# A transformer layer with 16384 experts: pools of its own for the first half of the expert blocks

## The chip, the cores and the metric

The kernel runs on one core of a Trainium2 chip. The metric is the device time of one execution in microseconds (us). Engines are named as in the profile: PE (TensorE; PEld is its weight load), DVE (VectorE), ACT (ScalarE), POOL (GpSimd) and SP (SyncE, here only an issuer of DMAs).

## The reference, cut to what matters

One layer over 1024 tokens of width 1024: two kinds of attention, an output projection, a LayerNorm, then PEER, a layer of 16384 experts of one neuron each, and a second LayerNorm. The change lies in PEER:

```python
def peer(x, w_q, sub_keys, u, v):
    q = (xf @ w_q).reshape(n, PEER_HEADS, 2, PEER_QDIM // 2)
    sc = jnp.einsum('nhpc,hpkc->nhpk', q, sub_keys)
    s_top, i_top = lax.top_k(sc, PEER_TOPK)                 # 16 of 128 keys, twice per head
    ...                                                     # 16 of the 16 x 16 sums
    g = jax.nn.softmax(fs, axis=-1)
    h = jnp.einsum('cd,chkd->chk', xc, u[ec])
    a = jax.nn.gelu(h, approximate=False) * gc
    return jnp.einsum('chk,chkd->cd', a, v[ec])
```

## The kernel before, in words

The tokens lie in eight tiles of 128. Attention, projection and LayerNorm run pair by pair of tiles, each pair followed by `route(pr)`, which finds the experts of its two tiles: transposes of x1 (L529) into `th` and `tl` (L530, L531; an fp32 value is carried as a high and a low half, so that a product takes three matmuls), then 16 steps over c, each with 24 matmuls into the PSUM tile `pq` (L555 to L557), a copy `q` (L559), two matmuls with the keys (L562), a copy `sc` (L564) and the selection of 16 on DVE. Each step loads its halves of the query weights by SP (`qhi`, L551). `decode` then works out expert numbers and gates on DVE (L179 to L235; `eidx` L224).

PEER itself is computed in two ways. **Tiles 5 to 7 are gathered**: 384 gathers by POOL (L656), each followed by a dot product (L658) and an accumulation (L668) on DVE. **Tiles 0 to 4 (640 tokens) are computed densely** over all experts, in 128 blocks of 128. Their gates must first stand in DRAM as a full table: POOL scatters those of tiles 0 and 1 (L165, into `gs`), and `build` makes those of tiles 2 to 4 by matmuls of one-hot rows (`pi`, `qj`, `pr`, `stage`, L602 to L617, into `gd`).

A dense block e is `hstage`: load `raw` from `ut[e]` (L709), split it into `uh` (ACT, L86) and `ul` (DVE, L87), 48 matmuls 128x320 in two runs of 24 into the one PSUM tile `h` (L91 to L93), a gelu of each run into `gl` (ACT, L718), a product of `gl` with the gates `gt` (DVE, L722), a split into `ah` and `al`, a load of `vt` into `raw` and its split into `vh` and `vl`. Then follow 18 matmuls 128x512 into `po` for tiles 0 to 2 (`vres`) and, for two blocks together, 24 into `fl` for tiles 3 and 4 (`vflush`), added to `facc` on DVE (L760, L765). `pump` spreads the gathers over the blocks.

The program text is not the order of the work. A scheduler (Tile) places each instruction in its engine's queue by its own estimate of times, and an engine runs its queue in order. What it may move is limited by buffers: the pool `dn` and the PSUM pool `ph`, which hold everything of the dense stage, take space that the pools of attention and `route` (closed by `late.close()` and the end of their block) held until then.

```python
    dn = ctx.enter_context(tc.tile_pool(name="dn", bufs=2))
    ph = ctx.enter_context(tc.tile_pool(name="ph", bufs=1, space=PSUM))
    ...
        raw = dn.tile([P, KT, P], F32, name="raw", bufs=3)
    ...
        gl = dn.tile([P, DN], F32, name="gl")
```

Of the kernel before, what the change touches and what calls it, by code (L numbers as in the profile page):

```python
# [11 lines left out]
F32 = mybir.dt.float32  # L12
F32R = mybir.dt.float32r
# [6 lines left out]
PSUM = bass.MemoryType.PSUM  # L20

P = 128
S = 1024
D = 1024
KT = D // P
# [11 lines left out]
GBUF = 4  # L37
ND = 5
NG = NT - ND
DN = ND * P  # L40
# [17 lines left out]
def trunk(ctx, tc, x, xt, wqk, wo, gn, sink, biasa, biasb, ln, wq, keyst, uv, ut, vt, out):  # L58
# [22 lines left out]
    def load_ln(g):  # L81
        for i in range(2):
            nc.scalar.dma_start(lnt[:, i, :], bcast_rows(ln[2 * g + i], D))

    def split(hi, lo, raw, lo_eng=None):
        cp = nc.scalar.copy(hi, raw)  # L86
        nc.vector.tensor_sub(lo, raw, f(hi))  # L87
        return cp

    def mm3(ps, wh, wl, mh, ml, first, last):  # L90
        nc.tensor.matmul(ps, wh, mh, start=first, stop=False)  # L91
        nc.tensor.matmul(ps, wh, ml, start=False, stop=False)  # L92
        nc.tensor.matmul(ps, wl, mh, start=False, stop=last)  # L93
# [538 lines left out]
    dl = dx.tile([P, KT, DN], F32R, name="dl")  # L632
    nc.sync.dma_start(f(dh), xd[0])
    nc.sync.dma_start(f(dl), xd[1])
    x1p = ctx.enter_context(tc.tile_pool(name="x1p", bufs=2, side="right"))
    x1 = {}
    load_ln(1)
    gp = ctx.enter_context(tc.tile_pool(name="gp", bufs=GBUF, side="right"))
    ga = ctx.enter_context(tc.tile_pool(name="ga", bufs=1, side="right"))
    sm = ctx.enter_context(tc.tile_pool(name="sm", bufs=2))  # L640

    def residual_ln(t, r, tmp):
# [35 lines left out]
    def pump(n):  # L678
        while n > 0 and done[0] < total:
            next(gen)  # L680
            done[0] += 1
            n -= 1

    dn = ctx.enter_context(tc.tile_pool(name="dn", bufs=2))
    ph = ctx.enter_context(tc.tile_pool(name="ph", bufs=1, space=PSUM))
    RES = 3
    po = [ph.tile([P, 2, 512], F32, name=f"po{c}") for c in range(RES)]
# [3 lines left out]
    xr = {}  # L691
# [4 lines left out]
    def load_g(g):  # L696
        gt[g] = dn.tile([P, DN // GC, EG, GC], F32, name="gt")
        sl = slice(g * EG, (g + 1) * EG)
        ns = NS * P // GC
        ld = nc.sync.dma_start(gt[g][:, 0:ns], gv[:, :, sl, :].rearrange("q j i c -> j q i c"))  # L700
        for t in range(NS):
            for b in added[t, 7]:
                tc.add_manual_dep(ld.ins, b.name, SYNC, reason="gates of every head")
        if NS < ND:
            nc.sync.dma_start(gt[g][:, ns:], gd[:, :, sl, :].rearrange("q j i c -> j q i c"))

    def hstage(e, pend):
        raw = dn.tile([P, KT, P], F32, name="raw", bufs=3)
        nc.sync.dma_start(raw, ut[e])  # L709
        uh = dn.tile([P, KT, P], F32R, name="uh")  # L710
        ul = dn.tile([P, KT, P], F32R, name="ul")
        split(uh, ul, raw)
        gl = dn.tile([P, DN], F32, name="gl")
        for j, (o, n) in enumerate(hch):
            ps = ph.tile([P, 512], F32, name="h")
            for k in range(KT):
                mm3(ps[:, :n], uh[:, k, :], ul[:, k, :], dh[:, k, o:o + n], dl[:, k, o:o + n], k == 0, k == KT - 1)
            nc.scalar.activation(gl[:, o:o + n], ps[:, :n], AF.Gelu)  # L718
            if j == (e == ne - 1) and pend is not None:
                vres(*pend)  # L720
        glv = gl.rearrange("p (q c) -> p q c", c=GC)
        nc.vector.tensor_mul(glv, glv, gt[e // EG][:, :, e % EG, :])  # L722
        ah = dn.tile([P, DN], F32R, name="ah", bufs=3)
        al = dn.tile([P, DN], F32R, name="al", bufs=3)
        split(ah, al, gl)
        raw = dn.tile([P, D], F32, name="raw", bufs=3)
        nc.sync.dma_start(raw, vt[e * P:(e + 1) * P, :])
        vh = dn.tile([P, D], F32R, name="vh", bufs=3)
        vl = dn.tile([P, D], F32R, name="vl", bufs=3)
        split(vh, vl, raw)  # L730
        return ah, al, vh, vl

    def vmm(ps, c, j, a, first, last):
        ah, al, vh, vl = a
        cs, js = slice(c * P, (c + 1) * P), slice(j * 512, (j + 1) * 512)
        nc.tensor.matmul(ps, ah[:, cs], vh[:, js], start=first, stop=False)  # L736
        nc.tensor.matmul(ps, ah[:, cs], vl[:, js], start=False, stop=False)  # L737
        nc.tensor.matmul(ps, al[:, cs], vh[:, js], start=False, stop=last)  # L738
# [3 lines left out]
    def vres(e, a):  # L742
        for c in range(RES):
            for j in range(2):
                vmm(po[c][:, j, :], c, j, a, e == 0, e == ne - 1)

    def vflush(e, a):
        prev.append(a)
        if len(prev) == 2:
            for c in range(RES, ND):  # L750
                acc = facc[c - RES]
                if e == 1:
                    xr[c] = dn.tile([P, D], F32, name="raw", bufs=3)
                    nc.scalar.dma_start(xr[c], xs[c])
                for j in range(2):
                    ps = ph.tile([P, 512], F32, name="fl")
                    for n, b in enumerate(prev):
                        vmm(ps, c, j, b, n == 0, n == 1)
                    if e == 1:
                        nc.vector.scalar_tensor_tensor(acc[:, j, :], xr[c][:, j * 512:(j + 1) * 512], ALPHA, ps,  # L760
                                                       op0=OP.mult, op1=OP.add)
                    else:
                        fl = dn.tile([P, 512], F32, name="fl", bufs=2)
                        nc.scalar.copy(fl, ps)  # L764
                        nc.vector.tensor_add(acc[:, j, :], acc[:, j, :], fl)  # L765
            prev.clear()

    fed = 0
    pend = None
    load_g(0)  # L770
    for e in range(ne):
        if e % EG == 0 and e + EG < ne:
            load_g(e // EG + 1)
        a = hstage(e, pend)
        if pend is not None:
            vflush(*pend)
        pend = (e, a)
        while fed < min(total, total * (e + 4) // ne):
            pump(1)
            fed += 1  # L780
    vres(*pend)
    vflush(*pend)
    pump(total)
    for c in range(ND):
# [78 lines left out]
```

## Time and profile before

| | us |
|---|---|
| median of 3 runs (lowest to highest) | 2982.5 (2979.24 to 2985.24) |
| the profiled execution | 2985.32 |
| its span in the trace | 2981.6 |
| PE busy / DVE busy / ACT busy / POOL busy | 2733.9 / 2408.1 / 1202.3 / 1065.1 |
| first matmul into `h` starts | 1133.34 |
| last matmul ends | 2961.9 |

The profiled execution's own time is 3.7 above its span. Busy time says how long an engine executed something, not whether anyone waited for it; for that the views of waits, the chain that ended last and the timelines are read, stage by stage. Times of instructions count from the start of the span.

### The profile page before, as it was taken

The page shows a single profiled execution, that of the slowest core. Times are in us where ns is not written, and L with a number is a line of the kernel's source. Part 1 is how long each engine was busy: PE and PEld are TensorE (multiplying, and loading weights), DVE is VectorE, ACT ScalarE, POOL GpSimd, SP SyncE. Part 2 cuts the span into 40 slices and gives each one's busy share as a digit, 9 for nine tenths or more (in the row PEclk, how much of TensorE's full clock was granted, in tenths as well). Part 3 has the DMA queues.
Part 4 walks back from the last instruction along what each step waited for, and adds up shares of the span by engine and source line. Part 5 has one row for each costly group of instructions (what it writes and reads, how often), then busy time and mean ns, then how long its engine had stood idle before and what let it go on. Part 6 is the DMA issues. An engine that isn't in the chain of part 4 may idle for free.

```text
span 2981.6 us, 43327 instructions
## 1 busy us (share of the span) xinstructions
PE 2733.9 (92%) x15569; PEld 2357.3 (79%) x15569; DVE 2408.1 (81%) x5427; ACT 1202.3 (40%) x2486; POOL 1065.1 (36%) x732
## 2 busy tenths in 40 slices
PE   6887899897997867999999999999999999999996
PEld 4776577575785766888998899898888898988885
DVE  2344267887979988898998989999989999998965
ACT  2343154342786762333333343333333333333332
POOL 1111001078888881333333323333333333333300
PEclk8998989898997988999999999999999999999998
DMA  7688598897977767988998989998998898998851
GB/s 233 200 271 269 177 322 296 260 262 180 267 223 221 220 161 265 348 331 324 353 331 332 332 329 335 336 347 334 330 344 327 321 353 322 342 349 332 329 210 46
DMA packets 384886, 854.37 MB, mean 287 GB/s; under 512 B 83616, under 2 KB 243360, under 8 KB 333728
## 3 DMA queue, kind: packets, MB, share of 16 engines
q0 software_dynamic: 124224, 433.43, 41.3%
q1 hardware_dynamic: 230816, 388.82, 38.5%
q10 hardware_dynamic: 29632, 29.37, 3.1%
q8 instruction: 122, 2.00, 0.3%
q14 instruction: 92, 0.75, 0.1%
HBM read 765.21 MB, written 86.11 MB: 286 GB/s over the span
## 4 chain that ended last, share of the span: by engine, by line
PE 48%; DVE 5%; DMA 4%; issue 3%; ACT 2%; POOL 1%; SPq 0%; ACTq 0%; POOLq 0%; DVEq 0%
PE h L91 9%; PE h L92 8%; PE h L93 8%; PE po L736 5%; PE po L737 5%; PE po L738 5%; PE fl L737 3%; PE fl L736 3%; PE fl L738 3%; DMA uv<-in_uv_dram,eidx 2%; DMA raw<-in_ut_dram 2%; DVE uv L658 1%; DVE acc L668 1%; POOL uv L656 1%; DVE vl L87 1%
## 5 line engine op out<-in xcount | busy, mean ns | idle before, releaser
L656 POOL DMA_INDIRECT uv<-in_uv_dram,eidx x384 | 570.4, 1486 | 1162.5 <-DVE acc L668 688.5
L91 PE MATMUL h<-dh,uh 128*128 128x320 f32 x2048 | 641.3, 313 | 49.0 <-ACT uh L86 25.6
L93 PE MATMUL h<-dh,ul 128*128 128x320 f32 x2048 | 634.6, 310 | 0.8 <-DVE ul L87 0.8
L92 PE MATMUL h<-dl,uh 128*128 128x320 f32 x2048 | 634.1, 310 | 0.0
L658 DVE SCALAR_TENSOR_TENSOR uv<-uv,xg 128x1024 f32<-128x1024 f32 x384 | 467.4, 1218 | 43.1 <-DMA uv<-in_uv_dram,eidx 37.3
L165 POOL DMA_INDIRECT gs<-gated,idxd x256 | 434.9, 1699 | 171.3 <-DMA qlo<-wqd 87.0
L668 DVE SCALAR_TENSOR_TENSOR acc<-uv,hh,acc 128x1024 f32<-128x1024 f32 x381 | 487.6, 1280 | 4.3
L91 PEld LDWEIGHTS h<-dh,uh 128*128 128x128 f32 x2048 | 385.7, 188 | 83.7 <-ACT gl L718 48.6
L92 PEld LDWEIGHTS h<-dl,uh 128*128 128x128 f32 x2048 | 385.9, 188 | 10.9
L93 PEld LDWEIGHTS h<-dh,ul 128*128 128x128 f32 x2048 | 385.7, 188 | 4.9 <-DVE ul L87 1.5
L736 PE MATMUL po<-vh,ah 128*128 128x512 f32 x768 | 288.2, 391 | 1.5 <-ACT ah L86 1.5
L737 PE MATMUL po<-vl,ah 128*128 128x512 f32 x768 | 287.8, 391 | 0.0
L662 ACT ACTIVATE hh<-hh 128x1 f32<-128x1 f32 x384 | 77.6, 202 | 476.3 <-DVE uv L658 474.9
L738 PE MATMUL po<-vh,al 128*128 128x512 f32 x768 | 260.8, 391 | 0.0
L764 ACT COPY fl<-fl 128x512 f32<-128x512 f32 x252 | 147.1, 584 | 278.7 <-PE fl L738 278.5
L765 DVE TENSOR_TENSOR facc<-facc,fl 128x512 f32<-128x512 f32 x252 | 172.6, 685 | 72.8 <-ACT fl L764 72.6
L718 ACT ACTIVATE gl<-h 128x320 f32<-128x320 f32 x256 | 111.4, 435 | 254.5 <-PE h L93 244.4
L736 PE MATMUL fl<-vh,ah 128*128 128x512 f32 x512 | 201.8, 394 | 3.0 <-ACT fl L764 3.0
L737 PE MATMUL fl<-vl,ah 128*128 128x512 f32 x512 | 201.9, 394 | 0.0
L738 PE MATMUL fl<-vh,al 128*128 128x512 f32 x512 | 199.6, 390 | 0.0
L87 DVE TENSOR_TENSOR ul<-raw,uh 128x1024 fp32r<-128x1024 f32 x128 | 156.1, 1220 | 52.6 <-ACT uh L86 51.7
L86 ACT CAST uh<-raw 128x1024 fp32r<-128x1024 f32 x128 | 134.2, 1049 | 116.8 <-DMA raw<-in_ut_dram 60.7
(201 smaller groups left out, 5389.2 us busy)
## 6 DMA issues: line engine op xcount, KB each, us to landing
raw<-in_ut_dram SPq DMA_DIRECT2D x128, 512.0 KB
raw<-in_vt_dram SPq DMA_DIRECT2D x128, 512.0 KB
qhi<-wqd SPq DMA_DIRECT2D x48, 512.0 KB
qlo<-wqd SPq DMA_DIRECT2D x48, 512.0 KB
gd<-stage SPq DMA_DIRECT2D x12, 2048.0 KB
gt<-gd SPq DMA_DIRECT2D x32, 768.0 KB
wraw<-in_wqk_dram SPq DMA_DIRECT2D x36, 512.0 KB
bt<-in_biasb_dram SPq DMA_DIRECT2D x64, 288.0 KB
```

Source lines behind the costliest of these rows:

```text
L87: nc.vector.tensor_sub(lo, raw, f(hi))
L91: nc.tensor.matmul(ps, wh, mh, start=first, stop=False)
L92: nc.tensor.matmul(ps, wh, ml, start=False, stop=False)
L93: nc.tensor.matmul(ps, wl, mh, start=False, stop=last)
L165: st = nc.gpsimd.indirect_dma_start(out=gs, out_offset=bass.IndirectOffsetOnAxis(ap=idx[:, k:k + 1], axis=0), in_=g[:, k:k + 1], in_offset ...
L656: nc.gpsimd.indirect_dma_start(out=u, out_offset=None, in_=uv, in_offset=bass.IndirectOffsetOnAxis(ap=eidx[t][:, k:k + 1], axis=0))
L658: nc.vector.scalar_tensor_tensor(u[:, 0:D], u[:, 0:D], 1.0, x1[t], op0=OP.mult, op1=OP.mult, accum_out=hh[:, k:k + 1])
L668: nc.vector.scalar_tensor_tensor(acc, u[:, D:], hh[:, k:k + 1], acc, op0=OP.mult, op1=OP.add)
L736: nc.tensor.matmul(ps, ah[:, cs], vh[:, js], start=first, stop=False)
L737: nc.tensor.matmul(ps, ah[:, cs], vl[:, js], start=False, stop=False)
L738: nc.tensor.matmul(ps, al[:, cs], vh[:, js], start=False, stop=last)
L765: nc.vector.tensor_add(acc[:, j, :], acc[:, j, :], fl)
```

## The change

The loads of `ut`, the halves `uh` and `ul` and the gelu results `gl` go from `dn` into a pool `du` that is allocated right behind `dh` and `dl` (the halves of the dense tiles' x, which are loaded behind `route(2)`; `load_ln` and the rest of the dense stage follow in the text), and the sums `h` go into a PSUM pool `hb` of one bank, both ahead of the remaining pools. `gl` has three buffers in place of two; `raw` has three as before. The four other pools get `reuse_waits="tile"`: a tile waits for the earlier tiles whose space it takes, not for the whole of the earlier pool. The first load of `ut` is written ahead of the gates' first load, and later gate loads behind `hstage`.

```diff
--- before.py
+++ after.py
@@ -632,11 +632,13 @@
     dl = dx.tile([P, KT, DN], F32R, name="dl")
     nc.sync.dma_start(f(dh), xd[0])
     nc.sync.dma_start(f(dl), xd[1])
-    x1p = ctx.enter_context(tc.tile_pool(name="x1p", bufs=2, side="right"))
+    du = ctx.enter_context(tc.tile_pool(name="du", bufs=2))
+    hb = ctx.enter_context(tc.tile_pool(name="hb", bufs=1, space=PSUM))
+    x1p = ctx.enter_context(tc.tile_pool(name="x1p", bufs=2, side="right", reuse_waits="tile"))
     x1 = {}
     load_ln(1)
-    gp = ctx.enter_context(tc.tile_pool(name="gp", bufs=GBUF, side="right"))
-    ga = ctx.enter_context(tc.tile_pool(name="ga", bufs=1, side="right"))
+    gp = ctx.enter_context(tc.tile_pool(name="gp", bufs=GBUF, side="right", reuse_waits="tile"))
+    ga = ctx.enter_context(tc.tile_pool(name="ga", bufs=1, side="right", reuse_waits="tile"))
     sm = ctx.enter_context(tc.tile_pool(name="sm", bufs=2))
 
     def residual_ln(t, r, tmp):
@@ -681,7 +683,7 @@
             done[0] += 1
             n -= 1
 
-    dn = ctx.enter_context(tc.tile_pool(name="dn", bufs=2))
+    dn = ctx.enter_context(tc.tile_pool(name="dn", bufs=2, reuse_waits="tile"))
     ph = ctx.enter_context(tc.tile_pool(name="ph", bufs=1, space=PSUM))
     RES = 3
     po = [ph.tile([P, 2, 512], F32, name=f"po{c}") for c in range(RES)]
@@ -704,15 +706,18 @@
         if NS < ND:
             nc.sync.dma_start(gt[g][:, ns:], gd[:, :, sl, :].rearrange("q j i c -> j q i c"))
 
-    def hstage(e, pend):
-        raw = dn.tile([P, KT, P], F32, name="raw", bufs=3)
+    def load_u(e):
+        raw = du.tile([P, KT, P], F32, name="raw", bufs=3)
         nc.sync.dma_start(raw, ut[e])
-        uh = dn.tile([P, KT, P], F32R, name="uh")
-        ul = dn.tile([P, KT, P], F32R, name="ul")
+        return raw
+
+    def hstage(e, pend, raw):
+        uh = du.tile([P, KT, P], F32R, name="uh")
+        ul = du.tile([P, KT, P], F32R, name="ul")
         split(uh, ul, raw)
-        gl = dn.tile([P, DN], F32, name="gl")
+        gl = du.tile([P, DN], F32, name="gl", bufs=3)
         for j, (o, n) in enumerate(hch):
-            ps = ph.tile([P, 512], F32, name="h")
+            ps = hb.tile([P, 512], F32, name="h")
             for k in range(KT):
                 mm3(ps[:, :n], uh[:, k, :], ul[:, k, :], dh[:, k, o:o + n], dl[:, k, o:o + n], k == 0, k == KT - 1)
             nc.scalar.activation(gl[:, o:o + n], ps[:, :n], AF.Gelu)
@@ -723,7 +728,7 @@
         ah = dn.tile([P, DN], F32R, name="ah", bufs=3)
         al = dn.tile([P, DN], F32R, name="al", bufs=3)
         split(ah, al, gl)
-        raw = dn.tile([P, D], F32, name="raw", bufs=3)
+        raw = du.tile([P, D], F32, name="raw", bufs=3)
         nc.sync.dma_start(raw, vt[e * P:(e + 1) * P, :])
         vh = dn.tile([P, D], F32R, name="vh", bufs=3)
         vl = dn.tile([P, D], F32R, name="vl", bufs=3)
@@ -750,7 +755,7 @@
             for c in range(RES, ND):
                 acc = facc[c - RES]
                 if e == 1:
-                    xr[c] = dn.tile([P, D], F32, name="raw", bufs=3)
+                    xr[c] = du.tile([P, D], F32, name="raw", bufs=3)
                     nc.scalar.dma_start(xr[c], xs[c])
                 for j in range(2):
                     ps = ph.tile([P, 512], F32, name="fl")
@@ -767,11 +772,12 @@
 
     fed = 0
     pend = None
+    first = load_u(0)
     load_g(0)
     for e in range(ne):
+        a = hstage(e, pend, load_u(e) if e else first)
         if e % EG == 0 and e + EG < ne:
             load_g(e // EG + 1)
-        a = hstage(e, pend)
         if pend is not None:
             vflush(*pend)
         pend = (e, a)
```

Three places show what this moves. The first is PE's queue at the start of `route(3)`: `x_10242` is the x1 of tile 6, whose transposes (L529) open that route; `pr` are the matmuls of `build`. Before:

```order
L615 MATMUL pr<-pi,qj 128x128 x35
L529 MATMUL pq<-ident,x_10242 128x128 x2
L615 MATMUL pr<-pi,qj 128x128
L529 MATMUL pq<-ident,x_10242 128x128 x2
L615 MATMUL pr<-pi,qj 128x128 x4
L529 MATMUL pq<-ident,x_10242 128x128 x4
L615 MATMUL pr<-pi,qj 128x128 x4
L529 MATMUL pq<-ident,x_10244 128x128 x4
L615 MATMUL pr<-pi,qj 128x128 x8
L529 MATMUL pq<-ident,x_10244 128x128 x4
```

Now:

```order
L615 MATMUL pr<-pi,qj 128x128 x28
L91 MATMUL h<-dh,uh 128x320
L92 MATMUL h<-dl,uh 128x320
L615 MATMUL pr<-pi,qj 128x128 x6
L529 MATMUL pq<-ident,x_10242 128x128 x4
L615 MATMUL pr<-pi,qj 128x128 x2
L93 MATMUL h<-dh,ul 128x320
L91 MATMUL h<-dh,uh 128x320
L92 MATMUL h<-dl,uh 128x320
L93 MATMUL h<-dh,ul 128x320
```

Matmuls into `h` (blocks 0 to 2, 144 in all) now stand between the transposes, the last 48 of them between the first and the third of the 16 steps over c; from the third step on both programs interleave `pr` and `pq` alike.

The second place is DVE's queue in the decode of tile 6 (L215 to L221 belong to it, L126 to L230 with numbers to tile 7's selection), shortly before the dense stage. Before:

```order
L215 TENSOR_TENSOR pf<-pf,of 128x128
L126 MATCH_REPLACE t_11330<-fs,cv 128x50
L126 MATCH_REPLACE t_11336<-fs,cv 128x50
L217 SCALAR_TENSOR_TENSOR big<-pf,fi 128x128 x8
L127 MAX fs<-t_11330 128x8
L127 MAX fs<-t_11336 128x8
L221 TENSOR_REDUCE ef<-big 128x128
L128 MAX_INDEX pos<-fs,t_11330 128x8
L128 MAX_INDEX pos<-fs,t_11336 128x8
L230 TENSOR_TENSOR gate_107<-fs 128x128
```

Now:

```order
L215 TENSOR_TENSOR pf<-pf,of 128x128
L87 TENSOR_TENSOR vl<-raw,vh 128x1024
L126 MATCH_REPLACE t_11330<-fs,cv 128x50
L126 MATCH_REPLACE t_11336<-fs,cv 128x50
L217 SCALAR_TENSOR_TENSOR big<-pf,fi 128x128 x8
L87 TENSOR_TENSOR vl<-raw,vh 128x1024
L127 MAX fs<-t_11330 128x8
L127 MAX fs<-t_11336 128x8
L87 TENSOR_TENSOR vl<-raw,vh 128x1024
L221 TENSOR_REDUCE ef<-big 128x128
L727 TENSOR_TENSOR gl<-gl,gt 128x640 x3
L128 MAX_INDEX pos<-fs,t_11330 128x8
```

The `vl` of blocks 0 to 2, the products of `gl` with the gates and the `al` have moved into this stretch; the `ul` of blocks 0 to 2, which followed some rows below, have gone to the start of `route(3)`.

The third place is PE's queue where the dense stage starts, behind the last 40 matmuls of `build`. Before:

```order
L615 MATMUL pr<-pi,qj 128x128 x3
L562 MATMUL pq<-kt,q 128x128 x2
L615 MATMUL pr<-pi,qj 128x128 x40
L91 MATMUL h<-dh,uh 128x320
L92 MATMUL h<-dl,uh 128x320
L93 MATMUL h<-dh,ul 128x320
```

Now:

```order
L615 MATMUL pr<-pi,qj 128x128 x3
L562 MATMUL pq<-kt,q 128x128 x2
L615 MATMUL pr<-pi,qj 128x128 x40
L741 MATMUL po_11454<-vh,ah 128x512
L742 MATMUL po_11454<-vl,ah 128x512
L741 MATMUL po_11455<-vh,ah 128x512
L742 MATMUL po_11455<-vl,ah 128x512
L741 MATMUL po_11456<-vh,ah 128x512
L742 MATMUL po_11456<-vl,ah 128x512
```

Where 72 matmuls into `h` stood first, `po` and `fl` of block 0 come first now. On SP, the loads `u`, `v`, `u` of blocks 0, 0 and 1 stand directly behind those of `dh` and `dl`, and `v`, `u`, `v` of blocks 1, 2 and 2 ahead of the `qhi` that `route(3)` loads for its third step (c = 2); the gate loads stand where they stood.

## Rows read from the trace of the kernel before

**Rows 1.** The page, part 1: engine, busy us, share, instructions.

```profile
PE 2733.9 (92%) x15569; PEld 2357.3 (79%) x15569; DVE 2408.1 (81%) x5427; ACT 1202.3 (40%) x2486; POOL 1065.1 (36%) x732
```

**Rows 2.** Windows: stretch, busy us per engine, granted clock, DMA share, GB/s.

```profile
940.00:980.00 40.00, 25.48 (x123) 22.91 (x123) 38.87 (x117) 29.82 (x68) 33.01 (x18) 0.60 0.57 157
980.00:1090.00 110.00, 91.89 (x713) 86.38 (x711) 94.53 (x368) 81.35 (x201) 93.96 (x53) 1.00 0.77 224
1110.00:1130.00 20.00, 0.00 (x0) 0.00 (x0) 20.00 (x99) 0.31 (x1) 5.83 (x4) 0.50 0.85 237
1200.00:2860.00 1660.00, 1640.02 (x9125) 1477.77 (x9124) 1515.49 (x2210) 595.24 (x1198) 554.17 (x372) 1.00 0.91 336
```

**Rows 3.** PE timeline, 1133 to 1164: start, us, instruction, idle before.

```profile
1133.34 0.64 PE L91 MATMUL h<-dh,uh 128*128 128x320 f32 x1 [25.65 <-ACT uh L86]
...
1139.04 0.47 PE L91 MATMUL h<-dh,uh 128*128 128x320 f32 x1
1139.30 0.42 PE L92 MATMUL h<-dl,uh 128*128 128x320 f32 x1
...
1139.70 0.31 PE L91 MATMUL h<-dh,uh 128*128 128x320 f32 x1
1139.85 0.31 PE L92 MATMUL h<-dl,uh 128*128 128x320 f32 x1
...
1149.59 0.39 PE L736 MATMUL po<-vh,ah 128*128 128x512 f32 x1
...
1154.38 0.30 PE L91 MATMUL h<-dh,uh 128*128 128x320 f32 x1
...
1163.24 0.39 PE L736 MATMUL po<-vh,ah 128*128 128x512 f32 x1
```

**Rows 4.** Chain that ended last, 1114 to 1133: start, us, what.

```profile
1114.59 4.18 DMA gs<-gated,idxd
1119.07 0.37 SPq L700
...
1124.24 7.67 DMA raw<-in_ut_dram
1132.25 1.05 ACT uh L86
```

**Rows 5.** DVE timeline, 1120 to 1149.

```profile
1120.09 0.26 DVE L215 TENSOR_TENSOR pf<-pf,of 128x128 f32<-128x128 f32 x1
...
1120.64 1.68 DVE L217 SCALAR_TENSOR_TENSOR big<-pf,fi 128x128 f32<-128x128 f32 x8
...
1122.49 1.84 DVE L221 TENSOR_REDUCE ef<-big 128x128 f32<-128x1024 f32 x1
...
1135.88 1.21 DVE L87 TENSOR_TENSOR vl<-raw,vh 128x1024 fp32r<-128x1024 f32 x1
...
1147.42 0.83 DVE L722 TENSOR_TENSOR gl<-gl,gt 128x640 f32<-128x640 f32 x1
```

**Rows 6.** ACT timeline, 969 to 971 and 1148.

```profile
969.64 1.28 ACT L231 ACT_TABLE_LOAD   x1
970.94 0.31 ACT L231 ACTIVATE gate<-gate 128x128 f32<-128x128 f32 x1
...
1148.28 0.73 ACT L86 CAST ah<-gl 128x640 fp32r<-128x640 f32 x1 [2.37 <-DVE gl L722]
```

**Rows 7.** PE waits, 930 to 980: for whom, us, times, longest.

```profile
PE pr L615 <- ACT qj L611: 16.5, 9, 5.7
```

**Rows 8.** PE timeline, first steps of route(3).

```profile
977.76 0.36 PE L555 MATMUL pq<-th,qhi 128*128 128x256 f32 x1
...
989.70 0.38 PE L555 MATMUL pq<-th,qhi 128*128 128x256 f32 x1 [0.46 <-ACT sc L564]
```

**Rows 9.** PE waits, 1200 to 2860.

```profile
PE h L91 <- ACT gl L718: 18.3, 32, 2.0
```

**Rows 10.** The page, part 5: DVE waiting for gathered rows.

```profile
L658 DVE SCALAR_TENSOR_TENSOR uv<-uv,xg 128x1024 f32<-128x1024 f32 x384 | 467.4, 1218 | 43.1 <-DMA uv<-in_uv_dram,eidx 37.3
```

## Prediction

> **What bounds the kernel now.** The page first: PE is busy 2733.9 of 2981.6 us [rows 1], so it is the engine to follow, and the question is where its other 248 us lie. The windows by stage tell that [rows 2]. From 1200 to 2860, over half of the run, PE is busy 1640.0 of 1660: the dense stage is bound by PE, and its idle 20.0 us are nearly all one wait, the first matmul of a run of 24 into `h` waiting for the gelu that empties the one `h` bank, 32 times, 18.3 us [rows 9], 0.57 each. Ahead of it PE does nothing at all in 1110 to 1130, while DVE is busy for all of it and PE's granted clock is 0.50 of full speed [rows 2]. In 940 to 980, where `route(3)` begins, PE is busy 25.5 of 40 us, DVE 38.9, ACT 29.8 [rows 2]; PE waits there 16.5 us for `qj`, which ACT scales [rows 7]. From 980 to 1090 PE is busy 91.9 of 110.
>
> The timeline shows the hole before the dense stage: the first matmul into `h` starts at 1133.34 after 25.65 idle, released by the split `uh` [rows 3]. The chain that ended last tells why it is so late [rows 4]: the last scatter of gates lands (4.18), SP then issues the gates' loads (1119.07), behind these in SP's queue the load of the first `u` (1124.24, 7.67 to its landing), then `uh` (1132.25, 1.05). Dense matmuls can't start before, though `dh`, `dl` and `u` need none of what `route(3)` computes: the buffers are what holds them.
>
> **What the change moves: the gain.** The matmuls into `h` of three blocks, 144, now stand in PE's queue at the start of `route(3)`; the dense stage opens with `po` and `fl`. A matmul into `h` takes 0.147 at full clock (1139.70 to 1139.85) and 0.267 at half (1139.04 to 1139.30) [rows 3]; three blocks are 144 x 0.147 = 21.2 us of PE's work.
>
> When can `po` of block 0 start? It needs `vl`, the gated `gl` and `ah`, which stand in DVE's queue behind L215 of tile 6's decode. In the trace of before L215 ends at 1120.35 [rows 5]. Behind it now stand, up to the first gated `gl`: three `vl` at 1.21 (3.63), the eight L217 (1.68), L221 (1.84), four short selections (0.3 and 0.2, the gaps between these in [rows 5]) and `gl` itself (0.83); then `ah` on ACT, 0.73 [rows 6]. Sum 9.2: `po` starts at 1129.6 + D, where D is by how much `route(3)` is delayed by the work put into it.
>
> What had PE done by when, before? Up to 1163.24 it did 120 matmuls into `h` (17.6 us) and 21 of 128x512 (1149.59 to 1154.38, 4.8) [rows 3], 22.4 in all, so 21.2 us of work stood done at 1162.0. The changed kernel has this much done when `po` starts, less one thing: its PE has idled and will start at the slow clock again. In before the first matmuls ran at 0.267 from 1133.3 to 1139.5, which gave away half of 6.2 us, 3.1 [rows 3]; I charge the same. DVE then has to finish tile 7's decode while PE runs 36 `po` and 6 `fl` (9.6 us, 12.7 with the cold start); going down both queues I find PE's needs (`al`, `ul` of block 3, the `facc` that free the `fl` bank) ready within a microsecond of PE's coming to them. So the start gains 1162.0 - 1129.6 - 3.1 - D = 29.3 - D.
>
> **What it costs: D.** Nothing in the trace shows matmuls into `h` between those of `route`, so D is bounded from both sides.
> - From below, only DVE: it is busy all but 1.1 us of 940 to 980, so three `ul` (1.2 each) come on top: 3.7.
> - From above, nothing overlaps: 21.2 us of matmuls and two more loads of ACT's tables (gelu, exp, gelu again), 1.28 each [rows 6]: 23.8.
> - Between them: 96 of the 144 matmuls stand ahead of the first step's, where PE idles 14.5 us of 40 [rows 2], most of it behind ACT [rows 7]. At full clock they are 14.1 us and fit; at the half clock that holds there they are 25.6. ACT gets three `uh` (3.2), four of the six gelus, and the two loads, about 7.5 us, against the 10.2 it has idle [rows 2]. Following the three queues by hand with these durations, the first step of `route(3)` (977.76) comes 4.5 later. The other 48 stand between it and the third step (989.70) [rows 8], where PE, busy 84% from 980 to 1090 [rows 2], has about 2 us idle: another 6. Behind that the queues are as before, and a step's pace is set by the exchange of PE and ACT, so I expect nothing back.
> D is 10.5, nearer to the lower bound. The start then gains 18.8.
>
> The loads of a table weigh most in this. By the rows the exp follows 1.30 after the load begins, with no gap. The Trainium skill ("ScalarE: Activation LUTs", section What ACT_TABLE_LOAD costs) states 1283 ns for the load and 1380 more for a drain, some 2.66 us a switch; the trace agrees with the first and shows nothing of the second here. By the page's figure two switches would be an estimated 2.8 us dearer, and the kernel would end 2.8 later.
>
> **The dense stage afterwards.** Each block has the same work. What differs is the order: counting in PE's queue, from the seventh block on, the places where a run into `h` follows another with at most three other matmuls between (too few to cover a gelu), before has 35 and the changed kernel 20. The trace has 32 waits for 35 such places, so I price each of the 15 fewer at 0.57: 8.6 gained. Bounds: 0 (the waits move elsewhere) and 18.3 (all go). The third `gl` and tile-wise waits add no work. The page's DMA and the tail behind the last matmul stay as they are: loads move 336 GB/s in the dense stage as before, 1 MB a block.
>
> **Sum.** 2985.3 - 18.8 - 8.6 = 2957.9 for an execution like the profiled one. That stood 2.8 above the median of the runs, which are 6.0 apart; against the median it is 2955.1. I take 2956.
>
> **The rivals.**
> 1. *The work in `route(3)` hides better*: the clock rises once PE has `h` to do, `pr` and `pq` run at the full clock too, and D is about 4. For it: 14.5 us of idle time at a granted clock of 0.60 [rows 2]. Against: DVE and ACT, which PE waits for, get work as well. Gain 25.3 + 8.6: about 2950.
> 2. *No gain in the dense stage*: the waits for gelu stay at 18.3. There is still one bank for `h`, and any run that follows another waits for it. Gain 18.8: 2966. The Trainium skill ("Perfetto Trace Analysis", section Optimizing Tensor Performance) asks that independent groups of matmuls rotate through banks, so that emptying one overlaps the next; by that rule one bank keeps the waits, as this rival has it, and [rows 9] bear it out for the old order alone.
> 3. *D eats the gain*: all of it serial, 23.8. The start gains 5.5: 2971 with the dense part, 2979 without, the latter no change that can be told.
> 4. *Slower: DVE falls behind.* DVE waits 37.3 us in all for gathered rows [rows 10], in order, with `gl`, `al` and `ul` queued behind. The first gather of tile 5 after the very first comes behind more DVE work than before, while PE stands three blocks ahead; if the queue makes DVE wait for gathers while PE waits for `ul`, each microsecond is PE's. It decides from 27 us of new waits, 33 for a loss that can be told; at 45, 3000. Against: DVE has 144 us idle from 1200 to 2860 [rows 2].
> 5. *It doesn't do what it says*: `po` comes no earlier than `h` came since the gates land late. Gates are issued at 1119.07 and 1119.49 and the next load lands by 1132, so at the worst `po` starts at 1133, later than 1129.6 + D only where D is under 3.4; the start then gains 25.9 and the kernel ends near 2948.
>
> **Chances and range.** Forecast (D 7 to 16, dense part 4 to 13) 0.52; rival 1 0.13; rival 2 0.15; rival 3 0.13, half of it within measurement; rival 4 0.06, rival 5 0.01. A difference of under 0.2%, 6 us, can't be told from none with runs 6 us apart. Faster by more: 0.52 + 0.13 + 0.15 + 0.05 = 0.85; the same 0.08; slower 0.07. The range goes from D = 4 with nearly all waits gone, 2982.5 - 25 - 16 = 2942, to rival 3 without the dense gain, 2978.
>
> **What would show it.** Right: matmuls into `h` in 940 to 990; the first `po` near 1140 with some 22 us of PE idle ahead; third step of `route(3)` near 1000; waits of `h` for `gl` near 10 us in 1200 to 2860; PE's end near 2934. Wrong: a third step past 1010 (rival 3); PE waiting for `ul`, `ah` or `facc` after the first `po` (rival 4); waits for `gl` at 18 (rival 2).

## The result, and the profile after

The changed kernel takes 2962.7 us (median; 2960.2 to 2964.4), before 2981.4 beside it: the ratio is 0.9944, interval 0.9928 to 0.9959, so 18.7 us faster. 26.5 were forecast (2982.5 to 2956); the time lies in the range. The profiled execution took 2960.2, its span is 2957.9. The page's first part, against [rows 1]:

```profile
PE 2721.2 (92%) x15569; PEld 2346.6 (79%) x15569; DVE 2407.4 (81%) x5427; ACT 1207.8 (41%) x2489; POOL 1070.8 (36%) x732
```

Times can't be held against those of before as they stand: what lies ahead of the change varies from execution to execution, whatever the kernel (the first load of the dense stage, `dh`, was issued between 917 and 933 in the profiles of this study). So positions are counted here **from the issue of `dh`**. That of before, from SP's timeline, and its last matmul of `build`, which ends 1107.69 - 928.36 = 179.3 behind it:

```profile
928.36 0.34 SPq L633 DMA_DIRECT2D dh<-xd  x1
```

```profile
1106.33 1.36 PE L615 MATMUL pr<-pi,qj 128*128 128x128 f32 x8 [0.63 <-ACT qj L611]
```

SP's timeline of the changed kernel: `dh`, then the loads of blocks 4 and 5 with the third group of gates between them.

```profile
924.73 0.34 SPq L633 DMA_DIRECT2D dh<-xd  x1
...
1162.95 0.33 SPq L732 DMA_DIRECT2D raw<-in_vt_dram  x1
1166.19 0.38 SPq L702 DMA_DIRECT2D gt<-gs  x1
1166.62 0.70 SPq L707 DMA_DIRECT2D gt<-gd  x1
1167.41 10.15 SPq L711 DMA_DIRECT2D raw<-in_ut_dram  x1
```

The windows of the changed kernel, in the order of [rows 2] (the third is its hole ahead of the dense stage):

```profile
940.00:980.00 40.00, 33.06 (x215) 31.66 (x215) 39.02 (x116) 34.46 (x68) 32.98 (x17) 0.83 0.70 201
980.00:1090.00 110.00, 94.46 (x742) 89.96 (x740) 90.40 (x345) 80.14 (x199) 93.63 (x54) 1.00 0.76 220
1115.00:1136.00 21.00, 0.09 (x1) 0.00 (x0) 17.92 (x68) 4.34 (x5) 1.01 (x1) 0.50 0.91 298
1200.00:2860.00 1660.00, 1645.84 (x9181) 1486.39 (x9180) 1526.20 (x2228) 601.15 (x1208) 564.21 (x376) 1.00 0.91 336
```

In 940 to 980 PE is busy for 33.1 us in place of 25.5, and its granted clock is 0.83 in place of 0.60. PE's timeline: the last `pr`, the first `po`, and a second hole.

```profile
1113.02 2.07 PE L615 MATMUL pr<-pi,qj 128*128 128x128 f32 x8 [2.24 <-ACT qj L611]
1136.42 0.80 PE L741 MATMUL po<-vh,ah 128*128 128x512 f32 x1 [21.33 <-ACT ah L86]
1137.02 0.63 PE L742 MATMUL po<-vl,ah 128*128 128x512 f32 x1
1137.44 0.63 PE L741 MATMUL po<-vh,ah 128*128 128x512 f32 x1
...
1142.01 0.40 PE L741 MATMUL po<-vh,ah 128*128 128x512 f32 x1
1142.24 0.40 PE L742 MATMUL po<-vl,ah 128*128 128x512 f32 x1
...
1184.03 0.64 PE L91 MATMUL h<-dh,uh 128*128 128x320 f32 x1 [6.29 <-ACT gl L723]
1184.46 0.47 PE L92 MATMUL h<-dl,uh 128*128 128x320 f32 x1
```

The last `pr` ends 190.4 behind `dh`, 11.0 later than before. The first `po` stands at 1136.42 - 924.73 = 211.7; before, the first `h` stood at 205.0. Matmuls of 128x512 come 0.43 apart until 1142 and 0.23 after: 2.6 us go to the cold clock (3.1 before). Then, at 1184, PE waits 6.29 us for a gelu and starts at 0.43 and 0.47 again.

DVE's timeline at the decode of tile 6, and ACT's:

```profile
1124.06 0.26 DVE L215 TENSOR_TENSOR pf<-pf,of 128x128 f32<-128x128 f32 x1
1127.41 1.23 DVE L87 TENSOR_TENSOR vl<-raw,vh 128x1024 fp32r<-128x1024 f32 x1 [3.08 <-ACT vh L86]
```

```profile
1115.13 1.05 ACT L616 COPY stage<-pr 128x512 f32<-128x512 f32 x1 [1.29 <-PE pr L615]
1126.33 2.94 ACT L86 CAST vh<-raw 128x1024 fp32r<-128x1024 f32 x3 [10.15 <-DMA gd<-stage]
...
1182.59 1.04 ACT L86 CAST uh<-raw 128x1024 fp32r<-128x1024 f32 x1 [13.37 <-DMA raw<-in_ut_dram]
1183.54 0.43 ACT L723 ACTIVATE gl<-h 128x320 f32<-128x320 f32 x1
```

And the two transfers behind these idle times, as the chain that ended last has them:

```profile
1116.20 10.05 DMA gd<-stage
...
1167.41 15.16 DMA raw<-in_ut_dram
```

The first `vh` waits 10.15 us for the write of the last `stage` tile, whose space it takes, and DVE 3.08 for `vh`. Near 1183 the gelu that PE waits for stands in ACT's queue behind `uh` of block 5, which waits 13.37 for its load: issued at 1167.41, landed 15.16 later. Meanwhile three gathers have just gone out, in POOL's timeline:

```profile
1162.06 1.69 POOL L658 DMA_INDIRECT uv<-in_uv_dram,eidx  x1 [45.68 <-DVE big L217]
1164.06 0.94 POOL L658 DMA_INDIRECT uv<-in_uv_dram,eidx  x1 [0.30 <-issue]
1165.30 1.88 POOL L658 DMA_INDIRECT uv<-in_uv_dram,eidx  x1 [0.31 <-issue]
```

In the dense stage, against [rows 9], the wait for the gelu is shorter:

```profile
PE h L91 <- ACT gl L723: 11.8, 19, 1.5
```

### The profile page after: what moved, and what is told of

It is laid out like the page before. It is cut to its first block, busy times and chain, and to the rows that moved or that the text cites. A ratio compares the mean times of both kernels' runs of the same rounds, so it can differ in the third digit from the quotient of the medians.

```text
span 2957.9 us, 43324 instructions
## 1 busy us (share of the span) xinstructions
PE 2721.2 (92%) x15569; PEld 2346.6 (79%) x15569; DVE 2407.4 (81%) x5427; ACT 1207.8 (41%) x2489; POOL 1070.8 (36%) x732
## 4 chain that ended last, share of the span: by engine, by line
PE 65%; DVE 14%; DMA 11%; issue 5%; ACT 5%; POOL 1%; ACTq 0%; SPq 0%; POOLq 0%; DVEq 0%
PE h L91 9%; PE h L93 9%; PE h L92 9%; PE po L741 5%; PE po L742 5%; PE po L743 5%; PE fl L742 3%; PE fl L741 3%; PE fl L743 3%; PE ps L483 3%; DMA gs<-zero 2%; DMA uv<-in_uv_dram,eidx 2%; DMA gd<-stage 1%; PE pq L555 1%; PE y L360 1%
## 5 line engine op out<-in xcount | busy, mean ns | idle before, releaser
L741 PEld LDWEIGHTS po<-vh,ah 128*128 128x128 f32 x768 | 144.5, 188 | 52.6 <-ACT ah L86 23.8
```

## The experiments

The table has all of them. Positions are those of the profiled execution, counted from `dh`; "done" is the number of matmuls into `h` ahead of the first `po`; the wait is that of PE in `h` for the gelu from 1200 to 2860. The lead says how far PE is ahead of before 300 us behind `dh`: the matmuls into `h`, `po` and `fl` that its timelines show begun by then, at 0.147 and 0.230 us each, an estimate good to about 1 us. Each position and lead comes from one profile. Ratios are to the kernel before on the same chip.

| kernel | last `pr` ends | first `po` (done) | lead at 300 | last matmul ends | wait for gelu | median us | ratio (interval) |
|---|---|---|---|---|---|---|---|
| before | 179.3 | 221.2 (72) | 0 | 2033.5 | 18.3 (32) | 2981.4 | 1 |
| changed | 190.4 | 211.7 (144) | 10.6 | 2013.9 | 11.8 (19) | 2962.7 | 0.9944 (0.9928 to 0.9959) |
| a0_again | 193.6 | 216.0 (144) | 6.7 | 2018.3 | 12.5 (19) | 2963.3 | 0.9940 (0.9921 to 0.9960) |
| e1_tile | 179.2 | 220.7 (72) | 1.4 | 2038.9 | 24.9 (36) | 2982.9 | 1.0003 (0.9988 to 1.0018) |
| e2_pools | 194.2 | 214.2 (144) | 12.7 | 2014.9 | 14.5 (20) | 2955.5 | 0.9903 (0.9875 to 0.9931) |
| e3_gl2 | 194.5 | 214.4 (120) | 3.8 | 2026.6 | 15.1 (26) | 2974.0 | 0.9976 (0.9957 to 0.9996) |
| e4_gl1 | 185.2 | 203.8 (72) | 8.4 | 2153.6 | 31.1 (47) | 3106.2 | 1.0401 (1.0378 to 1.0424) |
| e8_dv | 192.5 | 212.2 (144) | 10.1 | 2020.6 | 15.7 (22) | 2963.1 | 0.9938 (0.9915 to 0.9961) |
| e6_xr | 194.0 | 215.7 (144) | -29.0 | 2080.0 | 16.7 (25) | 3025.4 | 1.0152 (1.0119 to 1.0185) |
| e9_dvxr | 193.7 | 212.0 (144) | -29.0 | 2076.3 | 15.3 (25) | 3027.7 | 1.0161 (1.0128 to 1.0194) |
| e10_one | 186.9 | 206.7 (120) | 11.2 | 2028.6 | 19.2 (25) | 2968.6 | 0.9964 (0.9950 to 0.9977) |
| e11_xr | 193.8 | 216.5 (144) | 15.1 | 2006.6 | 10.3 (19) | 2953.6 | 0.9912 (0.9897 to 0.9927) |
| e12_both | 187.2 | 205.9 (120) | 18.7 | 2007.3 | 12.0 (19) | 2957.9 | 0.9925 (0.9911 to 0.9939) |
| e13_nohb | 190.5 | 214.2 (96) | 6.5 | 2026.7 | 16.5 (21) | 2965.1 | 0.9946 (0.9925 to 0.9968) |

**Tile-wise waits or pools.** e1_tile is before with this edit, on all four pools, alone:

```diff
+    x1p, gp, ga, dn: ..., reuse_waits="tile")
```

> The kernel before with the tile-wise waits of x1p, gp, ga and dn alone; every engine's queue is in the order of before. Theory (the gain comes from matmuls into h moved ahead of the hole, thus from the two pools): no change beyond 4 us of before, first matmul into h near 1133 again, since the first load of u still stands in SP's queue behind the gate loads, which wait for the last scatter. Rival (the gain comes from not waiting for whole pools): 10 us or more faster than before.

No change, 1.0003, and the dense stage starts where it did, 204.2 behind `dh`. Its waits for the gelu, in the order of before, show how far these vary by themselves (18.3 in [rows 9]):

```profile
PE h L91 <- ACT gl L718: 24.9, 36, 2.3
```

e2_pools is the opposite, the changed kernel without that edit:

```diff
-    x1p, gp, ga, dn: ..., reuse_waits="tile")
+    x1p, gp, ga, dn: ...)
```

> The changed kernel without the tile-wise waits, so the two pools and the third gl alone; every queue is in the order of the changed kernel. Theory: most of the 18.7 us stay, 2960 to 2970; the first po within 5 us of 1136. Rival (tile-wise waits carry the gain): back to 2975 or more, the first po held until old transfers have all landed.

The gain stays, 25.4 us (0.9903): the pools and the third `gl` carry it. Whether the tile-wise waits cost something isn't settled. In time e2_pools and a0_again (0.9940) stand 0.0037 apart, by intervals of 0.0028 and 0.0020, at the edge of what these runs can tell; the runs of e2_pools lie 25 us apart, and its profiled execution is one of the two slowest (2967.18), with its last matmul no sooner than that of the changed kernel. The first `po`, expected within 5 us of 1136, stands at 1145.02, by the count from `dh` 2.5 later. POOL, SP and PE of e2_pools, at the place of the second hole:

```profile
1177.75 1.90 POOL L658 DMA_INDIRECT uv<-in_uv_dram,eidx  x1 [62.34 <-DVE al L87]
```

```profile
1175.88 2.28 SPq L711 DMA_DIRECT2D raw<-in_ut_dram  x1
```

```profile
1188.54 0.41 PE L91 MATMUL h<-dh,uh 128*128 128x320 f32 x1 [2.24 <-ACT gl L723]
...
1189.46 0.63 PE L93 MATMUL h<-dh,ul 128*128 128x320 f32 x1 [0.36 <-DVE ul L87]
```

The gathers of tile 5 now wait until 1177.75, after the load of `u` of block 5 (1175.88), which in the changed kernel goes out behind three of them. The load lands 11.2 us after its issue; behind the gathers it took 15.1 to 15.3 (changed, a0_again, e8_dv). PE waits 2.24 there in place of 6.29, but in part because it comes there later, and 0.9 us on it runs cold as well (0.63 at 1189.46). It goes on 257.7 behind `dh`, 259.3 in the changed kernel and 263.8 in a0_again.

**How many blocks go ahead.** The number of `gl` buffers limits it.

```diff
-        gl = du.tile([P, DN], F32, name="gl", bufs=3)
+        gl = du.tile([P, DN], F32, name="gl", bufs=1)    # e4_gl1; e3_gl2: bufs=2
```

> The changed kernel with one gl buffer, so one block of matmuls into h goes ahead of the hole instead of three. Theory (each block moved ahead saves its 7.06 us of PE work if the hole ends no later): po starts near 1136, PE then has 7 us of work done, which before had near 1144: 4 to 7 us faster than before at the start, and the gelu now has one buffer, so the dense stage may lose some of it: 2972 to 2980. Rival (what counts is the earlier first load, not the number of blocks): the same as the changed kernel, 2960 to 2966.

In time e4_gl1 tells nothing on this: with one `gl` the whole dense stage waits, and the kernel is 125 us slower. PE's waits from 1200 to 2860:

```profile
PE po L743 <- DVE al L87: 47.8, 34, 4.4
PE h L91 <- ACT gl L723: 31.1, 47, 1.4
PE po L741 <- ACT ah L86: 22.5, 15, 3.2
```

Its start does tell something: with 72 matmuls done, `po` comes at 203.8, and at 300 us PE leads by 8.4, as much as with 144 done (10.6 and 6.7).

> The changed kernel with two gl buffers, so two blocks go ahead. Theory: 14.1 us of PE work stand done when po starts near 1136, before had this near 1153: 12 to 15 us gained at the start, 2966 to 2970, or as fast as the changed kernel (2960 to 2965) if the new hole near 1180, where PE waits behind a load of u, is not there, since PE then comes to it one block later. Rival (what counts is the earlier first load): as the changed kernel with the same hole.

e3_gl2 gains 6.9 (interval 1 to 13), less than either expectation has, though its interval reaches the theory's 12. Its first `po` stands as late as in the changed kernel, with 24 matmuls less done, and PE waits 4.75 for an `ah` at 1184.

**The late start.** a0_again is the changed kernel once more, so that the others have it beside them.

> The changed kernel once more, beside the other kernels of this call, since the chips and the early stages differ by some us from call to call. Theory: 16 to 26 us faster than before; counted from the issue of the dh load, the last pr ends 11 later than before's, the first po stands at 212, and between 1165 and 1190 PE waits 4 to 7 us for a gelu that stands behind a late load of u.

It gains 17.8; the last `pr` is 14.3 later and the first `po` stands at 216.0, 4 us later than in the first profile; the second hole is there with 6.39.

e8_dv gives `vh` and `vl` a pool of their own:

```diff
+    dv = ctx.enter_context(tc.tile_pool(name="dv", bufs=3, reuse_waits="tile"))
     dn = ctx.enter_context(tc.tile_pool(name="dn", bufs=2, reuse_waits="tile"))
...
-        vh = dn.tile([P, D], F32R, name="vh", bufs=3)
-        vl = dn.tile([P, D], F32R, name="vl", bufs=3)
+        vh = dv.tile([P, D], F32R, name="vh", bufs=3)
+        vl = dv.tile([P, D], F32R, name="vl", bufs=3)
```

> The changed kernel with vh and vl in a pool of their own ahead of dn, so that the first vh no longer lies where the last stage tile lay; the order of every queue is as in the changed kernel. Theory (DVE idles 3.1 us for the first vl because vh waits 10 us for the write of the last stage tile): the first po comes 3 us sooner, 2 to 4 us faster than the changed kernel. Rival (that wait is covered: po then waits for the gates instead, or the later hole takes it up): no difference.

In time it can't be told from a0_again (0.9938 and 0.9940); the 2 to 4 us of the theory lie within these intervals, so it isn't decided. In the profile DVE no longer waits for `vh` (3.08 and 4.19 us in the two profiles of the changed kernel), but now for the gates, 1.42:

```profile
1131.43 1.23 DVE L87 TENSOR_TENSOR vl<-raw,vh 128x1024 fp32r<-128x1024 f32 x1
...
1140.33 2.30 DVE L728 TENSOR_TENSOR gl<-gl,gt 128x640 f32<-128x640 f32 x3 [1.42 <-DMA gt<-gd]
```

These are the gates of tiles 2 to 4, read from what the last `stage` tile wrote: the last `pr`, 11 to 15 us later than before, then a copy, some 10 us of write and the gates' load. So that write stands behind both waits, and with the first taken away the second is left. From L215 to the first `po` the two profiles of the changed kernel take 12.4 and 13.4, e8_dv 10.7, and e9_dvxr (below), which has this edit and meets neither wait, 9.3. Most of the late start is L215 itself, 9.8 later than before in e8_dv.

**The second hole.** The two rows `xr` hold two of the three `raw` buffers from the start of the dense stage to the last of the four `facc`. e6_xr puts them elsewhere, e9_dvxr is that with e8_dv:

```diff
-                    xr[c] = du.tile([P, D], F32, name="raw", bufs=3)
+                    xr[c] = gp.tile([P, 2 * D], F32, name="uv")[:, 0:D]
```

> The changed kernel with the two rows of x for tiles 3 and 4 (xr) in buffers of the gathers instead of two of the three raw buffers, so that loads of u and v for blocks 3 to 5 go out some 20 us sooner. Theory (the new hole near 1180 is the load of u for block 5, issued at 1167 since raw was taken, and landing after 15): the hole is gone, with the cold clock behind it 5 to 9 us faster than the changed kernel, less some for a longer run of h behind h. Rival (the hole is DMA traffic of the gates and gathers, not the issue): the hole moves but stays.

> Both of these edits together. Theory: 7 to 12 us faster than the changed kernel, 28 to 36 faster than before. Rival: as the changed kernel.

Both lose 45 us, for a reason of my edit: `uv` buffers are handed out in the order of the program, so that `xr` comes behind the gathers written ahead of it (in e6_xr its loads are issued at 1212.53 and 1216.44), and PE stands still for the sum that needs it. So they can't tell the theory from its rival:

```profile
1219.59 0.79 PE L741 MATMUL fl<-vh,ah 128*128 128x512 f32 x1 [40.25 <-DVE facc L765]
```

e11_xr takes `xr` out of the start instead (a constant, 65, is written out here):

```diff
-                if e == 1:
+                if e == 65:
                     xr[c] = du.tile([P, D], F32, name="raw", bufs=3)
...
                     if e == 1:
-                        nc.vector.scalar_tensor_tensor(acc[:, j, :], xr[c]..., ALPHA, ps, ...)
+                        nc.scalar.copy(acc[:, j, :], ps)
                     else:
+                        if e == 65:
+                            nc.vector.scalar_tensor_tensor(acc[:, j, :], xr[c]..., ALPHA, acc[:, j, :], ...)
```

> The changed kernel, but the first sum of tiles 3 and 4 is copied into facc by ACT, and alpha times x is added at block 65: the two rows of x no longer hold two of the three raw buffers when the dense stage starts. It adds four additions of 128x512 on DVE and moves two loads. Theory (the hole near 1185, a gelu queued behind the split of a u that was issued late since raw was taken): the wait of 6.3 us and the cold clock behind it are gone, 5 to 9 us faster than the changed kernel, 2954 to 2958. Rival (the hole comes of DMA traffic of the gates and the first gathers): it stays, no difference.

As the theory had it: 0.9912, 25.5 us faster than before and the fastest median here. SP's timeline has the loads of `u` of blocks 4 and 5 at 1139 and 1152 (1155.76 and 1167.41 in the changed kernel, 1162.65 and 1174.26 in a0_again), and the hole is gone, though the start is as late as ever (216.5). With the same start as a0_again (216.0), PE leads by 15.1 at 300 us in place of 6.7. PE's waits for the gelu, from 1100 to 1200 and from 1200 to 2860:

```profile
1139.27 0.33 SPq L711 DMA_DIRECT2D raw<-in_ut_dram  x1
...
1152.33 0.33 SPq L711 DMA_DIRECT2D raw<-in_ut_dram  x1
```

```profile
PE h L91 <- ACT gl L723: 0.3, 1, 0.3
...
PE h L91 <- ACT gl L723: 10.3, 19, 1.1
```

**Is the PSUM pool needed?** e10_one lets one gelu result go ahead, e12_both is that with the edit of e11_xr, e13_nohb takes `hb` out:

```diff
-        gl = du.tile([P, DN], F32, name="gl", bufs=3)
+        gl = (dn if e else du).tile([P, DN], F32, name="gl", bufs=2 if e else 1)     # e10_one, e12_both
...
-    hb = ctx.enter_context(tc.tile_pool(name="hb", bufs=1, space=PSUM))              # e13_nohb
-            ps = hb.tile([P, 512], F32, name="h")
+            ps = ph.tile([P, 512], F32, name="h")
```

> The changed kernel with the gelu result of block 0 in du (one buffer) and those of all later blocks in dn (two buffers): 72 matmuls into h go into route(3) in place of 144, and 48 more stand in PE's queue right behind the last pr, in the hole itself. Theory (work in route(3) delays it by some 12 us for 144 matmuls, while the hole is free): the last pr ends 5 to 7 later than before's, counted from dh, the first po starts near 205 from dh, 8 us sooner than in the changed kernel, with 120 matmuls done, 24 fewer (3.5 us): 3 to 6 us faster than the changed kernel, 20 to 25 faster than before. Rival (what counts is how many blocks are moved into route(3)): about half the gain, 2970 to 2974.

The positions came near what was expected (last `pr` 7.5 later, `po` at 206.7), the time did not: 10.5 us faster than before, about half the gain, as the rival had it. But it isn't lost where the rival has it: at 300 us the lead is 11.2, no less than with 144 done. PE does use the hole, but from a cold start and with a wait between the two runs:

```profile
1114.98 0.64 PE L91 MATMUL h<-dh,uh 128*128 128x320 f32 x1 [3.74 <-ACT gl L723]
...
1125.38 0.64 PE L91 MATMUL h<-dh,uh 128*128 128x320 f32 x1 [4.49 <-ACT gl L723]
```

At 1172.62 it waits 4.76 for an `ah`, as e3_gl2 does. The rest went to the dense stage, with 19.2 us of waits for the gelu where the changed kernel has 12.

> Both of these edits. Theory: 8 to 14 us faster than the changed kernel, 2949 to 2955. Rival: the parts don't add up, since the first takes PE to the late load later: as the better of the two.

Both together reach 0.9925, which is not told apart from e11_xr: by the medians the parts don't add up. At 300 us its lead is 18.7, 3.6 more than that of e11_xr; at the last matmul nothing of this is left (2007.3 and 2006.6).

> The changed kernel without the PSUM pool hb: h lies in ph again, so no matmul into h can run before the PSUM tiles of route(3) are released, but the loads and splits of u for blocks 0 and 1 go ahead as in the changed kernel. In PE's queue 96 matmuls into h stand right behind the last pr, in the hole. Theory A (matmuls into h within route(3) cost it 11 to 15 us for the 21 they save, the hole is free): the last pr ends 2 to 5 later than before's, counted from dh, the first h starts within 6 us of it, the first po stands near 205 with 14.1 us of work done, and the whole is as fast as the changed kernel or up to 5 us faster, 2958 to 2964. Theory B (filling the idle places of route(3) is what pays): a third of the gain is lost, 2968 or more.

Without `hb` no matmul into `h` lies in `route(3)`: its first step stands where it stood before (49.4 behind `dh` in both), its last 1.9 sooner (147.7 and 149.6), and L215 comes 0.9 later. The last `pr`, though, ends 190.5 behind `dh`, 11.2 later than before and not 2 to 5: PE's timeline shows some 96 matmuls of `build` behind the last step, where before has 80. So this kernel differs from the changed one by more than the place of `h`. 96 matmuls into `h` then come ahead of `po`, the first of them warm, with a cold stretch from 1117.4 to 1120.6 behind the second wait:

```profile
916.87 0.34 SPq L633 DMA_DIRECT2D dh<-xd  x1
```

```profile
1103.55 3.85 PE L615 MATMUL pr<-pi,qj 128*128 128x128 f32 x16 [1.32 <-ACT qj L611]
1108.51 0.42 PE L91 MATMUL h<-dh,uh 128*128 128x320 f32 x1 [1.12 <-ACT stage L616]
...
1116.48 0.42 PE L91 MATMUL h<-dh,uh 128*128 128x320 f32 x1 [4.19 <-ACT gl L722]
...
1131.08 0.39 PE L740 MATMUL po<-vh,ah 128*128 128x512 f32 x1
```

The time, 0.9946, is that of the changed kernel, between the figures of both theories, so the gain doesn't need `hb`. The first `po` stands at 214.2, not near 205 as theory A had it. PE comes to it with 48 matmuls less done (7.1 us), but meets no second hole (6.3 and 2.6); at 300 us it leads by 6.5, as in a0_again. Beside e11_xr, which has neither loss, e13_nohb is slower by 0.0034, by intervals of 0.0015 and 0.0022.

## Why the prediction was right, and where its size was off

**The bound and the way** were right: three blocks of `h` ahead of the hole, PE busy behind it but for one more hole. By the count of matmuls begun, the changed kernel leads by 18.2 us at 240 behind `dh` (18.8 were forecast for the start), by 10.6 at 300, behind the second hole, and by 19.6 at the last matmul, so the dense stage gave 9.0 (8.6). In a0_again these are 15.4, 6.7 and 15.2. By the medians it is 18.7.

**D and the start.** D, put at 10.5, is by how much later L215 of tile 6 comes: 7.6 here (1124.06 - 924.73 = 199.3; before 1120.09 - 928.36 = 191.7), 9.8 to 11.5 in the other profiles in this order. The first step of `route(3)` was to be 4.5 later and is 2.6 (1 earlier on the clock, from an earlier `dh`), the third was to be 10.5 later and is 8.2. The last `pr` is 11.0 later, 13.2 to 14.9 in the other profiles. What rival 1 named is there in part: with `h` to do, PE's granted clock was 1.00 in 960 to 980, where before had 0.69. The first `po` was forecast at 1129.6 + 10.5, 211.7 behind `dh`, and stands at 211.7; 216.0 in the second profile. That it was hit is luck: L215 came 2.9 sooner than D has it, and behind it DVE waited 3.1 for `vh`, thus for the last `stage` write, which the sum put at nothing. Its chain behind L215 was right otherwise: 9.5 from the start of L215, 9.3 in e9_dvxr, which meets no such wait. The prediction also took the gates to land when they did before (rival 5); e8_dv shows that the late `pr` delays that write and so the gates of tiles 2 to 4.

**The tables of ACT** fit the rows again: 1.28 each, with the next instruction right behind where its data are there (966.29, then 967.59). The drain that the Trainium skill ("ScalarE: Activation LUTs", section What ACT_TABLE_LOAD costs) adds shows in no timeline here.

**The dense stage** was to gain 8.6. Waits fell by 6.5, and the count from 32 to 19; 15 fewer were forecast. Other profiles in the new order have 12.5, 14.5 and 15.7 (a0_again, e2_pools, e8_dv), e1_tile in the old one 24.9: the difference is 3 to 13, and its size isn't settled. e1_tile alone, with the queues of before, loses 6.8 us against before from 300 on, in its profile.

**The step that failed** is "I find PE's needs ... ready within a microsecond of PE's coming to them". The list of needs there (`al`, `ul` of block 3, `facc`) ends a block too soon: the `u` of block 5 came 6.3 us late, and the cold clock behind it (0.267 in place of 0.147 up to 1189) took 2.6, 8.9 in all. The two terms make 27.4; less 8.9 that is 18.5, against 18.7 measured. The lead falls there by 7.6, and by 8.7 in a0_again. e11_xr has the load earlier, loses no lead there and gains 25.5, near the 27.4 of a kernel without such a wait. So one cause of the hole is shown, `raw` buffers held by `xr`. The other, gathers that the tile-wise waits let out just ahead, is likely but not shown: the load landed 4 us faster in e2_pools, which goes ahead of them, but there PE also came later. How far each counts alone isn't told, as no kernel had both edits.

**The rivals' prices** do not stand on one footing: the forecast and rival 5 are taken from the median, rivals 2 and 3 from the profiled execution, 2985.3, so these two should be 2.8 less.

**Rival 4** named DVE falling behind the gathers. It didn't here: DVE's waits for gathered rows are 36.0 in all, 37.3 in [rows 10]. If the gathers cost PE time, then by the load of `u`.

## What to carry to other kernels

Where one stage idles for want of another's buffers, give the first instructions of the next stage space of their own, and then follow its loads two or three blocks further than the work moved: the next hole was a load whose buffers something else held. Work moved into a busy stage delays all that the stage feeds, here a write of gates by 11 to 15 us, half to two thirds of the 21.2 moved. More of it isn't better: 120 matmuls ahead led as much at 300 us as 144 (11.2 against 10.6 and 6.7; without the second hole 18.7 against 15.1; each from one profile). A kernel that left `route(3)` alone (e13_nohb) reached the same time. A weaker wait can let a transfer out ahead of one that is needed sooner, as it did the gathers here; what that cost these runs don't settle.

## What the runs showed of the hardware

The same 512 KB load took 7.67 us to land in [rows 4] and 15.16 behind 3 gathers and a group of gates, with a DMA share of 1.13 and 1.05 in the two stretches. The granted clock of 940 to 980 was 0.60 in [rows 2] and 0.83 with matmuls into `h` between those of `build`; in 960 to 980 it was 0.69 and 1.00, so those of `build` ran at the full level there too. And executions of one queue order differed by up to 4 us in the delay of `route(3)`, with `dh` itself moving by 16 between profiles; so positions want counting from a near event, and even then one profile of each can't tell an effect of 3 us.
